# Unsplit 32-bit input projections in a hybrid decoder step, with its parts in another order

## The chip, the cores and the metric

The kernel runs on one core of a Trainium2 chip. The metric is the device time of one execution in microseconds (us); times of a kernel are medians over several runs. The engines of the core are PE (matmul), DVE and POOL (elementwise), ACT (activations) and SP, whose queue issues most of the loads. Each engine takes its instructions strictly in the order in which the program lists them, and waits on semaphores for the others.

## The reference

One inference step of two decoder layers over 256 prompt tokens and 8 single-token samples, width 1024. Cut to what matters here:

```python
def _mixer(h, l, p, st):
    proj = h @ p['w_in'][l]                     # 1024 -> 2968 columns
    z, xbc, dt_raw, rw, gq, gk, gv, glo, gg = _split(proj, IN_SIZES)
    # SSD: causal conv of xbc over 4 tokens, silu, chunked scan, rmsnorm with silu(z)
    # RWKV-7: token shift of rw, decay, delta-rule recurrence, group norm, bonus, gate
    # GLA: log_sigmoid gate from glo, chunked scan, rmsnorm with silu(gg)
    y = jnp.concatenate([y_ssd, y_rwkv, y_gla], axis=-1) @ p['w_out'][l]
...
def _layer(x, c, l, p, st):
    mod = jax.nn.silu(c) @ p['w_ada'][l] + p['b_ada'][l]
    sh1, sc1, gt1, sh2, sc2, gt2 = [m[:, None, :] for m in jnp.split(mod, 6, axis=-1)]
    h = x * (1.0 + sc1) + sh1
    m, new_st = _mixer(h, l, p, st)
    x = _layernorm(ALPHA * x + (1.0 + gt1) * m, p['ln_mix_g'][l], p['ln_mix_b'][l])
    h = x * (1.0 + sc2) + sh2
    f = _swiglu(...) if l % 2 == 0 else _moe(...)
    x = _layernorm(ALPHA * x + (1.0 + gt2) * f, p['ln_ffn_g'][l], p['ln_ffn_b'][l])
    return x, new_st
```

## The kernel before

Activations lie feature by feature: a tile has 128 features in partitions and TT = 264 tokens (256 prompt, 8 samples) in columns, and `h` is four tiles of two such blocks. The stages follow one another: setup and the first `ada` blocks (to about 23 us), mixer of layer 0 (23 to 255), output projection (to about 292), dense FFN (299 to 502), mixer of layer 1 (502 to 697), output projection (to 735), router and experts (741 to 1110), final norm and output.

The large products are made of three fp32r matmuls. `block` (L380) loads a weight tile of 128 x 1024 as `w` through SP's queue (L384), copies it to fp32r on ACT (`wh`, L296) and subtracts that from it on DVE (`wl`, L317). `split` does the same for an activation (`hh`, `hl`). `mm3` (L392) then multiplies wh by hh, wh by hl and wl by hh into one PSUM bank. `tile_mm` (L626) does it for eight k-steps of 128.

In a mixer, `proj` (L680) makes 24 input projections per layer this way (PSUM tile `pj`, two banks): the tiles 0 to 7 are for RWKV, 8 to 13 for the conv of SSD, 14 to 17 for GLA, 18 to 23 for the gates z. Between them run the parts of the mixer: the RWKV chunk chain (`gr`, `pb`, `p`, ...), its single-token step (`rstep`, tiles `sr`, `srw`), its output (`rout`, L1037: `gm`, `gv`, `gn`, `gb`), SSD's preparation (`ssd_prep`, L1231: `ta`, `stk`, `tt`, and a trip through DRAM that comes back as `cu`, from which ACT makes `sd`), its step (`sstep`, L1382: `bx`, `sst`, `sss`), GLA. Interleaved with them, `ada` (L446) makes one block of the adaLN modulation: sixteen matmuls with `wa` tiles, an ACT copy `adae`, four transposes `adat`, and on DVE a reduction, an addition of the bias and sometimes a scaling.

What stands next to what is decided when the program is built. `ORDER` is the order in which a layer's parts are emitted; `LOW` shifts the priority of a named part, projection (`p3.1` is tile 3 of layer 1) or weight split; `FILL` says after which part or projection how many `ada` blocks are emitted. A scheduler turns this into one fixed list of instructions for each engine, so that matmuls of projections fall between the steps of the chains. Buffers are few: three for `w`, three each for `wh` and `wl`, two for `wa`, two PSUM banks for `pj`.

Of the kernel before, what the change touches and what calls it, by code (L numbers as in the profile page):

```python
# [166 lines left out]
def _unpack(r):  # L167
# [20 lines left out]
 'd': 'hh hl cv qk gv zs xo bl xg al',  # L188
# [4 lines left out]
T1 = {'u': 'gt xt x akt rt ee fs raw', 'r': 'vt st vb q1 ab', 'd': 'xb', 't': 'w ends ed sm da dx rs8 mx cslot'}  # L193
# [5 lines left out]
ORDER = [['rwkv', 'conv', 'rstep', 'qkv', 'aff', 'sstep', 'rout', 'gstep', 'gla', 'ssd', 'z2', 'gread', 'z1', 'z0'],  # L199
 ['rstep', 'rwkv', 'conv', 'sstep', 'qkv', 'rout', 'gstep', 'aff', 'gla', 'ssd', 'z0', 'z1', 'z2', 'gread']]  # L200
X = {'FR': 1, 'AHEAD': 1, 'SA': 4}
MOE = {'s0': 28, 'ss': 6, 'g0': 31, 'gs': 5, 'wa': 2, 'e0': 11, 'es': 5}
LOW = {'rout.0': -9440,
 'win.1': -20,
 'sstep.0': -1560,
 'z2.0': -640,
 'rwkv.0': 200,
 'ssd.0': -780,
 'rout.1': -1500,
 'p10.1': 1020,  # L210
 'p4.1': -20,
 'p17.1': -120,
 'sp.1': -20,
 'p0.1': -20,
 'conv.1': -200,
 'win.0': -20,
 'p0.0': -1560,
 'p6.1': -20,
 'gread.1': 100,
 'p16.0': 380,  # L220
 'p14.0': -60,
 'p8.1': -60,
 'fin.1': -60,
 'p19.1': -200,
 'p9.1': 1560,
 'p16.1': 20,
 'p6.0': -20,
 'p9.0': -20,
 'rstep.0': -140,
 'p8.0': -20,  # L230
 'p11.1': -20,
 'p22.0': 200,
 'gp.1': 20}
FILL = {'1.12': 1,
 '1.11': 1,
 '0.13': 1,
 '0.10': 1,
 '1.3': 1,
 '0.qkv': 2,
 '0.o5': 1,  # L240
 '1.z2': 1,
 '0.5': 1,
 '0.15': 1,
 '1.qkv': 1,
 '0.sstep': 1,
 '1.9': 1,
 '1.10': 1,
 '0.conv': 1,
 '0.gla': 1,
 '1.o5': 1,  # L250
 '0.ssd': 1,
 '1.o6': 1}
# [4 lines left out]
ROW = 0  # L257

# [8 lines left out]
class Net:  # L267
    def __init__(self, nc, tc, I, O, stack):
        self.nc, self.tc, self.I, self.O = nc, tc, I, O
        p = lambda name, bufs, **k: stack.enter_context(tc.tile_pool(name=name, bufs=bufs, **k))  # L270
        self.cp = p("const", 1)
        self.wp = p("wts", NW["w"])
        self.ap = p("wada", NW["a"])
        self.hp = p("whi", NW["h"])
        self.lp = p("wlo", NW["l"])
        self.bp = p("big", 1)
        self.p2 = {t: p("f2" + t, n) for t, n in N2.items()}
        self.p1 = {t: p("f1" + t, n) for t, n in N1.items()}
# [123 lines left out]
    def setup(self):  # L402
# [14 lines left out]
        for j in (1, 2, 4, 5):  # L417
            b = self.bada[:, :, j * 8:j * 8 + 8]
            self.ts(b, b, 1.0, OP.add)
# [26 lines left out]
    def ada(self, l, j, n, first=False):  # L446


        if True:
            ps = self.ps("ada")  # L450
            before = None
            for c in range(2):
                cs = slice(c * 256, c * 256 + 256)
                for kq in range(2):
# [6 lines left out]
                    else:  # L461
                        w = self.ap.tile([128, 4, 256], F32, tag="wa", name=f"wa_{self.n}")
                        self.nc.sync.dma_start(w, src)
# [11 lines left out]
            pt = self.ps("adat", [128, 4, 4, 32])  # L475
            for c in range(4):
                self.tr(pt[:, c].rearrange("p a b -> p (a b)"), ev[:, c * 128:c * 128 + 128])
            m = self.mod[:, l, j, n * 4:n * 4 + 4, :]
            self.nc.vector.tensor_reduce(m, pt[:, :, :, :9].rearrange("p c h b -> p c b h"), axis=AX.X, op=OP.add)
            b = self.bada[:, l, j * 8 + n * 4:j * 8 + n * 4 + 4]  # L480
            self.add(m, m, b[:, :, None].to_broadcast([128, 4, 9]))
            if j % 3 == 2:
                self.ts(m, m, 1.0 / ALPHA, OP.mult)
# [26 lines left out]
    def modulate(self, k, gb):  # L510

        gm, bm = gb
        h = self.f2("h")
# [48 lines left out]
    def norm(self, st, g, b, gb=None, keep=False, out=None):  # L562
# [28 lines left out]
        for k, x in zip(range(0, 8, 2), xs):  # L591
            h = self.f2("hk" if keep else "h")
# [40 lines left out]
    def out_proj(self, l, y):  # L633
# [10 lines left out]
        return self.norm(st, g, b, self.scales(l, 3, g, b), l == 1)  # L644

    def ffn(self, l, h):
# [30 lines left out]
        return self.norm(st, g, b, self.scales(l + 1, 0, g, b))  # L677
# [616 lines left out]
    def conv(self, l, h):  # L1294
# [128 lines left out]
    def run(self):  # L1423
        self.setup()
        h, gb = [], self.scales(0, 0)
        for n in range(2):
# [4 lines left out]
            if n == 0:  # L1431
                self.ahead = [self.block(self.I["win"][0, i]) for i in range(X["AHEAD"])]
# [282 lines left out]
```

## Time and profile before

| | us |
|---|---|
| median of 3 runs | 1121.98 |
| runs | 1121.74, 1128.61, 1121.98 |
| profiled execution | 1125.45 |
| its span | 1123.7 |
| PE busy (92%) | 1031.0 |
| DVE busy (66%) | 744.7 |
| ACT busy (54%) | 607.6 |

The mean granted clock of PE in the profiled execution was 0.961 of full speed. Engine time is the time in which the engine had an instruction in work. "Idle before" is the time for which an engine stood still before an instruction; the name after the arrow is the instruction or transfer that released it.

### The profile page before, as it was taken

To read this page: it belongs to the slowest core of one execution; us is meant where nothing else is said; L and a number is where in the kernel's file an instruction comes from. 1 tells how busy PE (TensorE), PEld (TensorE's weight loads), DVE (VectorE), ACT (ScalarE), POOL (GpSimd) and SP (SyncE) were. 2 spreads that over 40 slices of the span, in tenths; PEclk is the share of its full clock that TensorE was granted. 3 is DMA by queue.
4 is the path that set the end of the run, shared out by engine and by line. 5 is a ranking of instruction groups with operands and counts; after the bars stand their busy time and mean duration, and the time that the engine had idled before them with its cause. 6 is when DMAs were issued, how large, how long until landed. Compare 5 with 4: busy or idle time off the path is not lost. (4 is left out here: it accounts for less than half of the span.)

```text
span 1123.7 us, 22379 instructions
## 1 busy us (share of the span) xinstructions
PE 1031.0 (92%) x8912; PEld 833.5 (74%) x8912; DVE 744.7 (66%) x1406; ACT 607.6 (54%) x1037; POOL 87.1 (8%) x191
## 2 busy tenths in 40 slices
PE   6879997889899999999899998979999999999995
PEld 2668765557699999987677875858777777778663
DVE  1577646655665545457876876476788888878775
ACT  2656323254554444338653265357767766776663
POOL 1131112100100000001412210010000000000000
PEclk9999988699899999998999999989999999999998
DMA  9774468773465655555674454416889888988881
GB/s 354 266 220 147 132 205 242 264 232 118 151 194 181 186 176 178 150 169 175 217 226 156 145 170 149 158 43 208 300 296 304 299 286 300 306 291 288 287 280 42
DMA packets 71184, 238.55 MB, mean 212 GB/s; under 512 B 9280, under 2 KB 10016, under 8 KB 71072
## 3 DMA queue, kind: packets, MB, share of 16 engines
q1 hardware_dynamic: 66512, 226.18, 61.4%
q0 software_dynamic: 4000, 10.71, 3.5%
q8 instruction: 72, 1.18, 0.4%
q14 instruction: 40, 0.33, 0.1%
q10 hardware_dynamic: 560, 0.15, 0.1%
HBM read 231.50 MB, written 5.51 MB: 211 GB/s over the span
## 5 line engine op out<-in xcount | busy, mean ns | idle before, releaser
L317 DVE TENSOR_TENSOR wl<-w,wh 128x1024 fp32r<-128x1024 f32 (+1 forms) x324 | 388.7, 1215 | 157.6 <-ACT wh L296 155.5
L296 ACT ACTIVATE wh<-w 128x1024 fp32r<-128x1024 f32 (+1 forms) x324 | 334.2, 1051 | 272.4 <-issue 74.1
L336 PE MATMUL pj<-hh,wh 128*128 128x264 f32 x384 | 119.4, 313 | 7.6 <-ACT cv L296 3.3
L336 PE MATMUL pj<-hl,wh 128*128 128x264 f32 x384 | 120.4, 315 | 0.2 <-DVE hl L317 0.2
L336 PE MATMUL pj<-hh,wl 128*128 128x264 f32 x384 | 118.5, 310 | 1.4 <-DVE wl L317 1.3
L336 PEld LDWEIGHTS pj<-hh,wh 128*128 128x128 f32 x384 | 76.7, 201 | 22.0 <-issue 8.5
L336 PEld LDWEIGHTS pj<-hh,wl 128*128 128x128 f32 x384 | 77.0, 201 | 7.6 <-DVE wl L317 2.7
L336 PE MATMUL eg<-wh,xo 128*128 128x512 f32 x256 | 81.6, 395 | 0.2 <-ACT wh L296 0.2
L336 PEld LDWEIGHTS pj<-hl,wh 128*128 128x128 f32 x384 | 76.7, 200 | 6.7 <-issue 4.0
L336 PE MATMUL eg<-wh,xg 128*128 128x512 f32 x256 | 81.2, 395 | 0.4 <-ACT wh L296 0.4
L336 PE MATMUL ada<-wa,sc 128*32 128x256 f32 x640 | 55.0, 430 | 17.7 <-DMA wa<-in_wada 17.0
L336 PE MATMUL eg<-wl,xg 128*128 128x512 f32 x128 | 53.1, 415 | 5.3 <-DVE wl L317 5.1
L336 PE MATMUL ed<-wl,ath 128*128 128x512 f32 x128 | 52.6, 411 | 4.4 <-DVE wl L317 4.1
L336 PEld LDWEIGHTS eg<-wh,xg 128*128 128x128 f32 x256 | 48.1, 188 | 10.8 <-ACT wh L296 1.4
L336 PEld LDWEIGHTS eg<-wh,xo 128*128 128x128 f32 x256 | 48.1, 188 | 10.3 <-ACT wh L296 0.6
L336 PE MATMUL eg<-wl,xo 128*128 128x512 f32 x128 | 52.5, 410 | 1.5 <-DVE wl L317 1.4
L336 PE MATMUL ed<-wh,ath 128*128 128x512 f32 x128 | 50.9, 398 | 0.0
L336 PE MATMUL ed<-wh,atl 128*128 128x512 f32 x128 | 50.6, 395 | 0.0
L336 PE MATMUL fg<-hh,wh 128*128 128x264 f32 x176 | 50.4, 286 | 0.0
L336 PE MATMUL fu<-hl,wh 128*128 128x264 f32 x176 | 50.4, 286 | 0.0
L336 PE MATMUL fg<-hh,wl 128*128 128x264 f32 x176 | 50.2, 286 | 0.0
L336 PE MATMUL fg<-hl,wh 128*128 128x264 f32 x176 | 50.2, 286 | 0.0
(477 smaller groups left out, 2296.2 us busy)
## 6 DMA issues: line engine op xcount, KB each, us to landing
w<-in_moe SPq DMA_DIRECT2D x192, 512.0 KB, 4.6
wa<-in_wada SPq DMA_DIRECT2D x80, 512.0 KB, 4.5
w<-in_win SPq DMA_DIRECT2D x48, 512.0 KB, 4.6
w<-in_ffgu SPq DMA_DIRECT2D x44, 512.0 KB, 3.6
k<-in_wada SPq DMA_DIRECT2D x32, 256.0 KB, 5.8
w<-in_wout SPq DMA_DIRECT2D x16, 512.0 KB, 4.4
w<-in_ffd SPq DMA_DIRECT2D x16, 512.0 KB, 3.6
w<-in_ffd SPq DMA_DIRECT2D x8, 384.0 KB, 3.9
```

What stands on the lines that cost most here:

```text
L296: r = self.nc.scalar.activation(out, in_, func, bias=bias, scale=scale)
L317: return (e or self.nc.vector).tensor_tensor(out, a, b, op=op)
L336: return self.nc.tensor.matmul(out, lhsT, rhs, start=start, stop=stop)
```

## The change

The projections no longer split weights and input. `raw` loads a weight tile as it is, from the pool of `w`, and `proj` makes eight plain f32 matmuls of the f32 weights and the f32 `h`; `modulate` and the norm after the FFN return `h` unsplit. The other large products (output projection, FFN, experts) stay as they were. The four transposes of `ada` become four f32 matmuls with a 128 x 9 matrix `pick`, which do the sum that the DVE reduction did, and bias and scale are one DVE operation. In the conv, the products for the sample tokens (18 small DVE operations a layer) become one product, one reduction and three additions. In `affine` and the final norm, the product per feature block becomes one per pair, and the gain moves into ACT's scale. The tables ORDER, LOW and FILL have new values; the number of `ada` blocks is the same.

```diff
-ORDER = [['rwkv', 'conv', 'rstep', 'qkv', 'aff', 'sstep', 'rout', 'gstep', 'gla', 'ssd', 'z2', 'gread', 'z1', 'z0'],
- ['rstep', 'rwkv', 'conv', 'sstep', 'qkv', 'rout', 'gstep', 'aff', 'gla', 'ssd', 'z0', 'z1', 'z2', 'gread']]
+ORDER = [['rwkv', 'conv', 'rstep', 'qkv', 'aff', 'sstep', 'rout', 'gstep', 'gla', 'gread', 'ssd', 'z2', 'z1', 'z0'],
+ ['rstep', 'rwkv', 'conv', 'sstep', 'qkv', 'gstep', 'rout', 'aff', 'gla', 'ssd', 'z0', 'z1', 'gread', 'z2']]
...
-LOW = {'rout.0': -9440,
+LOW = {'conv.1': -200,
...
-FILL = {'1.12': 1,
+FILL = {'0.10': 1,
...
+RAW = {'a': 'a', 'p': 'w'}
...
+    def raw(self, src, ada=False):
+
+        self.n += 1
+        c = "a" if ada else "p"
+        kinds = RAW[c]
+        at = self.turn.get(c, 0)
+        self.turn[c] = at + 1
+        k = kinds[at % len(kinds)]
+        pool, tg = {"w": (self.wp, "w"), "a": (self.ap, "wa"), "h": (self.hp, "h"), "l": (self.lp, "l")}[k]
+        w = pool.tile([128, 1024], F32, tag=tg, name=f"w_{self.n}")
+        self.nc.sync.dma_start(w, src)
+        return w
...
-            self.ts(b, b, 1.0, OP.add)
+            self.ts(b, b, 1.0, OP.add, *((1.0 / ALPHA, OP.mult) if j % 3 == 2 else ()))
+        self.pick = cp.tile([128, 9], F32, name="pick")
+        nc.vector.tensor_reduce(self.pick, self.ident.rearrange("p (q b) -> p b q", q=4)[:, :9], axis=AX.X, op=OP.add)
         self.mod = cp.tile([128, L, 6, 8, 9], F32, name="mod")
...
-                        w = self.ap.tile([128, 4, 256], F32, tag="wa", name=f"wa_{self.n}")
-                        self.nc.sync.dma_start(w, src)
+                        w = self.raw(src, True).rearrange("p (a b) -> p a b", a=4)
                         ws = [w[:, :2], w[:, 2:]]
...
-            pt = self.ps("adat", [128, 4, 4, 32])
+            pt = self.ps("adat", [128, 4, 9])
             for c in range(4):
-                self.tr(pt[:, c].rearrange("p a b -> p (a b)"), ev[:, c * 128:c * 128 + 128])
+                self.mm(pt[:, c], ev[:, c * 128:c * 128 + 128], self.pick)
             m = self.mod[:, l, j, n * 4:n * 4 + 4, :]
-            self.nc.vector.tensor_reduce(m, pt[:, :, :, :9].rearrange("p c h b -> p c b h"), axis=AX.X, op=OP.add)
-            b = self.bada[:, l, j * 8 + n * 4:j * 8 + n * 4 + 4]
-            self.add(m, m, b[:, :, None].to_broadcast([128, 4, 9]))
+            b = self.bada[:, l, j * 8 + n * 4:j * 8 + n * 4 + 4, None].to_broadcast([128, 4, 9])
             if j % 3 == 2:
-                self.ts(m, m, 1.0 / ALPHA, OP.mult)
+                self.stt(m, pt, 1.0 / ALPHA, OP.mult, b, OP.add)
+            else:
+                self.add(m, pt, b)
...
-        h = self.f2("h")
+        h = self.f2("hw")
         self.act(h[:, 0, :T], self.x[:, k, :T], AF.Identity, scale=gm[:, k, 0:1], bias=bm[:, k, 0:1])
         self.ts(h[:, 1, :T], self.x[:, k + 1, :T], gm[:, k + 1, 0:1], OP.mult, bm[:, k + 1, 0:1], OP.add)
         self.mul(h[:, :, T:], self.x[:, k:k + 2, T:], gm[:, k:k + 2, 1:], self.nc.gpsimd)
         self.add(h[:, :, T:], h[:, :, T:], bm[:, k:k + 2, 1:], self.nc.gpsimd)
-        r = self.f2("hh", dt=F32R), self.f2("hl", dt=F32R)
-        self.split(r[0], r[1], h)
-        return r
+        return h
...
+                self.mul(y, y, r[:, None, :].to_broadcast([128, 2, TT]))
                 for i in range(2):
-                    self.stt(y[:, i], y[:, i], g[:, k + i:k + i + 1], OP.mult, r, OP.mult)
-                    self.act(y[:, i], y[:, i], AF.Identity, bias=b[:, k + i:k + i + 1])
+                    self.act(y[:, i], y[:, i], AF.Identity, scale=g[:, k + i:k + i + 1], bias=b[:, k + i:k + i + 1])
...
-            h = self.f2("hk" if keep else "h")
+            h = self.f2(keep or "h")
...
-            for k in range(8):
-                x = self.x[:, k]
-                both = self.stt(x, x, g[:, k:k + 1], OP.mult, r, OP.mult), self.act(x, x, AF.Identity, bias=b[:, k:k + 1])
+            for k in range(0, 8, 2):
+                x = self.x[:, k:k + 2]
+                both = [self.mul(x, x, r[:, None, :].to_broadcast([128, 2, TT]))]
+                for i in range(2):
+                    both.append(self.act(x[:, i], x[:, i], AF.Identity, scale=g[:, k + i:k + i + 1], bias=b[:, k + i:k + i + 1]))
...
     def proj(self, l, i, h):
         with self.low(f"p{i}.{l}"):
-            hi, lo = self.ahead.pop(0) if self.ahead else self.block(self.I["win"][l, i], by=f"win.{l}")
+            w = self.ahead.pop(0) if self.ahead else self.raw(self.I["win"][l, i])
             ps = self.ps("pj")[:, :TT]
-            self.tile_mm(ps, hi, lo, h)
+            for k in range(8):
+                self.mm(ps, w[:, k * 128:k * 128 + 128], h[k // 2][:, k % 2], k == 0, k == 7)
...
+        old, S3 = self.f1("cvt", [128, 6, NB]), [128, 6, 3, NB]
+        each = self.f1("cve", S3)
+        self.mul(each, scv, cw[:, :, :3, None].to_broadcast(S3))
+        nc.vector.tensor_reduce(old, each.rearrange("p t k b -> p t b k"), axis=AX.X, op=OP.add)
...
-                self.stt(yq[:, T:], scv[:, t, k], w(k), OP.mult, yq[:, T:], OP.add)
...
+                self.add(y[:, :, T:], y[:, :, T:], old[:, t - 1:t + 1])
...
-                self.ahead = [self.block(self.I["win"][0, i]) for i in range(X["AHEAD"])]
+                self.ahead = [self.raw(self.I["win"][0, i]) for i in range(X["AHEAD"])]
```

The new order shows on three engines. First ACT in mixer 0, at the r and v projections of RWKV; `tt` belongs to the preparation of SSD, `sd` needs the transfer `cu`, and `ab` goes to the RWKV chain. Before:

```order
L296 ACTIVATE v_468<-pj_705,omu 128x264
L296 ACTIVATE adae_683<-ada_658 128x512
L296 ACTIVATE raw_767<-pj_742 128x264
L296 ACTIVATE v_468<-pj_742,omu 128x264
L296 ACTIVATE ta_777<-ta_777 8x256
L296 ACTIVATE wh_1580<-w_1578 128x1024
L296 ACTIVATE tt_799<-stk_798 128x144
L296 ACTIVATE sd_806<-cu_805,tt_799 128x128 x4
L296 ACTIVATE lt_849<-lg_848 128x264
L296 ACTIVATE sd_806<-sd_806 128x512
L296 ACTIVATE lt_849<-lt_849 128x264
L296 ACTIVATE ab_869<-gr_894 128x128
```

After:

```order
L308 ACTIVATE b_465<-b_465 128x264 x2
L308 ACTIVATE tt_619<-stk_618 128x144
L308 ACTIVATE r_409<-pj_494,omu 128x264
L308 ACTIVATE r_409<-pj_511,omu 128x264
...
L308 ACTIVATE v_410<-pj_561,omu 128x264
L308 ACTIVATE raw_587<-pj_578 128x264
L308 ACTIVATE v_410<-pj_578,omu 128x264
L308 ACTIVATE sd_626<-cu_625,tt_619 128x128 x4
L308 ACTIVATE ab_689<-gr_714 128x128
```

`tt` stood behind the v projections, directly ahead of `sd`, and now stands ahead of both r and v; `sd` is still ahead of `ab`, by one place. Then DVE in mixer 0, where the step of SSD meets the output of RWKV; `sst` needs the transfer `bx`, and `gn` goes to PE for `gv` and `gb`. Before:

```order
L333 SCALAR_TENSOR_TENSOR o_589<-gm_2263,o_589 128x264
L317 TENSOR_TENSOR sss_2200<-sss_2200,da_844 128x512
L317 TENSOR_TENSOR sst_2175<-bx_2170,dx_2159 128x2x128 x2
L333 SCALAR_TENSOR_TENSOR gn_2261<-r_467,par,k_109_564 128x264
L317 TENSOR_TENSOR sss_2174<-sss_2174,sst_2175 128x512
L317 TENSOR_TENSOR wl_2962<-w_2959,wh_2961 128x1024
```

After:

```order
L345 SCALAR_TENSOR_TENSOR o_491<-gm_1862,o_491 128x264
L329 TENSOR_TENSOR sss_1801<-sss_1801,da_664 128x512
L345 SCALAR_TENSOR_TENSOR gn_1860<-r_409,par,k_101_466 128x264
L329 TENSOR_TENSOR sst_1776<-bx_1771,dx_1760 128x2x128 x2
L329 TENSOR_TENSOR sss_1775<-sss_1775,sst_1776 128x512
L329 TENSOR_TENSOR gn_1860<-gb_1872,v_410 128x264
```

`gn` stood behind `sst` and now stands ahead of it. Last SP's queue of loads in mixer 0, with what each load waits for (`w` are projection weights when they come from in_win, `wada` the weights of `ada`). Before:

```order
L384 DMA w_1491<-in_win 128x1024 [waits DMAHW5_49,DVE_49]
L384 DMA w_1533<-in_win 128x1024 [waits DMAHW7_49,DMAHW6_49,DVE_49]
L463 DMA wa_671<-in_wada 128x1024 [waits PE_49]
L463 DMA wa_677<-in_wada 128x1024 [waits DMAHW0_49,PE_49]
L463 DMA wa_1610<-in_wada 128x1024 [waits DMAHW7_49,DMAHW1_49,PE_49]
L384 DMA w_1578<-in_win 128x1024 [waits DMAHW2_49,DVE_49,Activation_49]
L463 DMA wa_1616<-in_wada 128x1024 [waits DMAHW3_49,DMAHW0_49,PE_49]
L384 DMA w_1655<-in_win 128x1024 [waits DMAHW4_49,DMAHW5_49,DVE_49,Activation_49]
L384 DMA w_1699<-in_win 128x1024 [waits DMAHW6_49,DVE_49,Activation_49]
```

After:

```order
L414 DMA w_1357<-in_win 128x1024 [waits DMAHW5_49,PE_49]
L414 DMA w_1409<-in_win 128x1024 [waits PE_49]
L414 DMA w_1431<-in_win 128x1024 [waits DMAHW7_49,DMAHW2_49,PE_49]
L414 DMA w_1450<-in_win 128x1024 [waits DMAHW5_49,PE_49]
L414 DMA w_1381<-in_wada 128x1024 [waits DMAHW1_49,PE_49]
L414 DMA w_1387<-in_wada 128x1024 [waits DMAHW3_49,PE_49]
L414 DMA w_1473<-in_wada 128x1024 [waits DMAHW1_49,PE_49]
L414 DMA w_1479<-in_wada 128x1024 [waits DMAHW4_49,DMAHW2_49,PE_49]
L414 DMA w_1613<-in_win 128x1024 [waits DMAHW6_49,PE_49]
```

A load of projection weights waited for DVE (and ACT), which had split the tile in its buffer, and now waits for PE, which has multiplied with it; the loads of `ada` are in the same queue, in groups, as before.

## Rows read from the trace of the kernel before

**Rows 1.** The page's first part: busy us, share of the span, instructions of an engine.

```profile
PE 1031.0 (92%) x8912; PEld 833.5 (74%) x8912; DVE 744.7 (66%) x1406; ACT 607.6 (54%) x1037; POOL 87.1 (8%) x191
```

**Rows 2.** Windows: width, busy us of PE, PEld, DVE, ACT, POOL, clock, DMA share, GB/s.

```profile
23.00:255.00 232.00, 204.32 (x2581) 152.66 (x2582) 140.76 (x344) 103.44 (x229) 35.41 (x69) 0.90 0.67 218
...
299.00:502.00 203.00, 203.00 (x1623) 196.99 (x1625) 109.24 (x160) 93.21 (x139) 0.00 (x0) 0.99 0.56 170
502.00:697.00 195.00, 178.58 (x2399) 142.26 (x2392) 147.12 (x364) 106.50 (x241) 40.12 (x76) 0.96 0.57 181
```

**Rows 3.** Waits of PE: its instruction <- releaser, us in total, times, longest.

```profile
PE ada L336 <- DMA wa<-in_wada: 17.0, 13, 3.5
...
PE adat L369 <- ACT adae L296: 5.4, 8, 0.8
...
PE pb L369 <- DVE x L317: 5.0, 1, 5.0
...
PE gb L336 <- DVE gn L333: 4.4, 1, 4.4
...
PE pj L336 <- ACT cv L296: 3.3, 1, 3.3
```

**Rows 4.** Timeline, all engines, at 78 us: start, us, engine, instruction [idle before <- releaser].

```profile
78.56 1.28 ACT L296 ACTIVATE sd<-cu,tt 128x128 f32<-128x128 f32 x4 [5.73 <-DMA cu<-ssdd]
...
80.89 0.25 ACT L296 ACTIVATE ab<-gr 128x128 f32<-128x128 f32 x1
...
81.25 0.29 DVE L317 TENSOR_TENSOR x<-gr,cst 128x128 f32<-128x128 f32 x1 [6.11 <-ACT ab L296]
...
81.59 0.48 PE L369 MATMUL pb<-ident,b 128*128 128x128 f32 x1 [5.01 <-DVE x L317]
```

**Rows 5.** Timeline, all engines, at 177 us.

```profile
176.92 0.76 DVE L317 TENSOR_TENSOR sst<-bx,dx 128x256 f32<-128x256 f32 x2 [4.69 <-DMA bx<-bcr_d]
...
178.14 0.81 PE L336 MATMUL gb<-gn,cst 128*128 128x264 f32 x1 [4.44 <-DVE gn L333]
```

**Rows 6.** Timeline of PE, at 50 and at 254 us.

```profile
49.75 0.28 PE L336 MATMUL pj<-hh,wl 128*128 128x264 f32 x1
...
53.90 0.28 PE L336 MATMUL pj<-hh,wh 128*128 128x264 f32 x1
...
254.05 1.05 PE L336 MATMUL ssq<-zs,onem 128*128 128x264 f32 x4
254.94 0.61 PE L336 MATMUL gn<-gsq,cst 128*128 128x264 f32 x2
```

**Rows 7.** The page's groups: busy us, mean ns of one | idle before.

```profile
L317 DVE TENSOR_TENSOR wl<-w,wh 128x1024 fp32r<-128x1024 f32 (+1 forms) x324 | 388.7, 1215 | 157.6 <-ACT wh L296 155.5
L296 ACT ACTIVATE wh<-w 128x1024 fp32r<-128x1024 f32 (+1 forms) x324 | 334.2, 1051 | 272.4 <-issue 74.1
```

**Rows 8.** Timeline, at 33 and (PE) at 760 us.

```profile
32.95 0.66 PE L369 MATMUL adat<-ident,adae 128*128 128x128 f32 x4 [0.76 <-ACT adae L296]
...
759.73 1.66 PE L336 MATMUL cs<-comb,sel 128*128 128x1 f32 x12
```

**Rows 9.** Timeline, all engines, at the start of mixer 0.

```profile
34.22 1.09 ACT L296 ACTIVATE h<-x,mod 128x256 f32<-128x256 f32 x2 [1.32 <-DVE mod L317]
...
35.22 1.16 ACT L296 ACTIVATE hh<-h 128x528 fp32r<-128x528 f32 x2
...
35.89 0.59 PE L336 MATMUL pj<-hh,wh 128*128 128x264 f32 x1 [2.29 <-ACT hh L296]
```

**Rows 10.** Loads: the page's DMA issues, the issuing line (ns, landing us), SP's waits.

```profile
w<-in_win SPq DMA_DIRECT2D x48, 512.0 KB, 4.6
...
L384 SPq DMA_DIRECT2D w<-in_win x48: 327/328/1538, 14.3 to 644.7; - x48
...
DMA to landing us min/median/max: 3.1/4.5/8.2
...
SPq L463 <- PE ada L336: 127.9, 57, 11.7
```

More of the change, by code (lines that the diff above doesn't have):

```diff
@@ L187 @@
 T2 = {'r': 'ai k r cs kk k2 ka rkt bk gn gr ah htl az',
- 'd': 'hh hl cv qk gv zs xo bl xg al',
+ 'd': 'hh hl hw cv qk gv zs xo bl xg al',
  'g': 'gqk gsc o hk sq rbt',
@@ L192 @@
  'm': 'srm srv bx sst sgu sgl gsq'}
-T1 = {'u': 'gt xt x akt rt ee fs raw', 'r': 'vt st vb q1 ab', 'd': 'xb', 't': 'w ends ed sm da dx rs8 mx cslot'}
+T1 = {'u': 'gt xt x akt rt ee fs raw', 'r': 'vt st vb q1 ab', 'd': 'xb', 't': 'w ends ed sm da dx rs8 mx cslot cvt'}
 TP = {'a': 'ada adat st',
@@ L198 @@
 N1 = {'r': 10, 'd': 2, 's': 8, 't': 13, 'u': 6}
-ORDER = [['rwkv', 'conv', 'rstep', 'qkv', 'aff', 'sstep', 'rout', 'gstep', 'gla', 'ssd', 'z2', 'gread', 'z1', 'z0'],
- ['rstep', 'rwkv', 'conv', 'sstep', 'qkv', 'rout', 'gstep', 'aff', 'gla', 'ssd', 'z0', 'z1', 'z2', 'gread']]
+ORDER = [['rwkv', 'conv', 'rstep', 'qkv', 'aff', 'sstep', 'rout', 'gstep', 'gla', 'gread', 'ssd', 'z2', 'z1', 'z0'],
+ ['rstep', 'rwkv', 'conv', 'sstep', 'qkv', 'gstep', 'rout', 'aff', 'gla', 'ssd', 'z0', 'z1', 'gread', 'z2']]
 X = {'FR': 1, 'AHEAD': 1, 'SA': 4}
-MOE = {'s0': 28, 'ss': 6, 'g0': 31, 'gs': 5, 'wa': 2, 'e0': 11, 'es': 5}
-LOW = {'rout.0': -9440,
- 'win.1': -20,
[L205 to L233, printed above, removed]
-FILL = {'1.12': 1,
[L235 to L241, printed above, removed]
- '0.5': 1,
[L243 to L247, printed above, removed]
+MOE = {'e0': 11, 'es': 5, 'g0': 31, 'gs': 5, 's0': 28, 'ss': 6, 'wa': 2}
+LOW = {'conv.1': -200,
+ 'fin.1': -80,
+ 'gp.1': 40,
+ 'gread.0': -600,
+ 'gread.1': 100,
+ 'p0.0': -1560,
+ 'p0.1': -20,
+ 'p10.1': 1020,
+ 'p11.1': -20,
+ 'p13.1': -1520,
+ 'p14.0': -60,
+ 'p14.1': 200,
+ 'p16.1': 20,
+ 'p17.1': -120,
+ 'p19.1': -200,
+ 'p21.0': 60,
+ 'p22.0': 200,
+ 'p4.1': -20,
+ 'p6.0': -20,
+ 'p6.1': -20,
+ 'p7.0': -600,
+ 'p8.0': -20,
+ 'p8.1': -60,
+ 'p9.0': -20,
+ 'p9.1': 1560,
+ 'rout.0': -9440,
+ 'rout.1': -1500,
+ 'rp.0': 60,
+ 'rp.1': 20,
+ 'rstep.0': -140,
+ 'rstep.1': 20,
+ 'rwkv.0': 200,
+ 'sp.1': -20,
+ 'ssd.0': -780,
+ 'sstep.0': -1560,
+ 'win.1': -20,
+ 'wout.1': -60,
+ 'z0.1': -20,
+ 'z1.1': -1500,
+ 'z2.0': -640}
+FILL = {'0.10': 1,
+ '0.15': 1,
+ '0.5': 1,
  '0.conv': 1,
  '0.gla': 1,
- '1.o5': 1,
+ '0.o5': 1,
+ '0.qkv': 2,
+ '0.rstep': 1,
  '0.ssd': 1,
- '1.o6': 1}
+ '0.sstep': 1,
+ '1.12': 1,
+ '1.18': 1,
+ '1.3': 1,
+ '1.9': 1,
+ '1.o4': 1,
+ '1.o6': 1,
+ '1.qkv': 1,
+ '1.ssd': 1,
+ '1.z1': 1,
+ '1.z2': 1}
 NW = {'w': 3, 'a': 2, 'h': 3, 'l': 3}
@@ L283, in __init__ @@
         self.setname = None
+        self.turn = {}
         self.pre = None
@@ L643, in out_proj @@
         g, b = self.P(l, "lnm_g"), self.P(l, "lnm_b")
-        return self.norm(st, g, b, self.scales(l, 3, g, b), l == 1)
+        return self.norm(st, g, b, self.scales(l, 3, g, b), "hk" if l == 1 else None)
     def ffn(self, l, h):
@@ L676, in ffn @@
         g, b = self.P(l, "lnf_g"), self.P(l, "lnf_b")
-        return self.norm(st, g, b, self.scales(l + 1, 0, g, b))
+        return self.norm(st, g, b, self.scales(l + 1, 0, g, b), "hw")
     def proj(self, l, i, h):
         with self.low(f"p{i}.{l}"):
-            hi, lo = self.ahead.pop(0) if self.ahead else self.block(self.I["win"][l, i], by=f"win.{l}")
+            w = self.ahead.pop(0) if self.ahead else self.raw(self.I["win"][l, i])
             ps = self.ps("pj")[:, :TT]
-            self.tile_mm(ps, hi, lo, h)
+            for k in range(8):
+                self.mm(ps, w[:, k * 128:k * 128 + 128], h[k // 2][:, k % 2], k == 0, k == 7)
         self.hook(l, i)
```

## The prediction

> **What bounds the kernel now.** I read the engine table first: TensorE (PE) is busy 92% of the span, and its weight loads 74% [rows 1]. Then the table by stage [rows 2]. In the dense FFN between the two mixers PE has no idle time at all (203.00 of 203.00 us), so nothing that the change does there could show, and it does almost nothing there. The two mixers are the only stages where PE both works hard and waits: in the first it is busy 204.3 of 232 us, in the second 178.6 of 195, which leaves 27.7 + 16.4 = 44.1 us idle, and the granted clock is 0.90 and 0.96 where the FFN has 0.99. All the projections lie in these stages. So the change is a trade on one engine: more matmul time in the mixers, against whatever part of the 44.1 us (and of the low clock) is caused by the work that it removes.
>
> Third, the list of PE's waits, to see what those 44.1 us are [rows 3]. The largest is not the projections at all but `ada` waiting for its own weights (17.0 us in 13 waits). Then come two single long stalls of 5.0 and 4.4 us, and small waits for ScalarE (ACT) and VectorE (DVE). The two long ones are worth following in the timeline. At 81.59 PE's transpose `pb` begins after 5.01 us idle; it waits for a DVE product that waits for `ab` on ACT; and ACT stood 5.73 us before `sd`, which needs `cu`, a DMA through DRAM of the SSD part [rows 4]. `ab` was ready to go and stood behind `sd`. The second is the same on DVE: `sst` waited 4.69 us for the DMA `bx`, and the product `gn`, which PE's `gb` needs, stood behind it [rows 5]. Both are head-of-line stalls of an in-order engine, not lack of throughput.
>
> **The change, part by part.** *Projections.* A product of three fp32r matmuls has its starts 122 ns apart (49.75 to 53.90 in 34 steps [rows 6]), so a k-step costs 366 ns and a tile of eight 2.93 us. The new product is one f32 matmul, which PE runs as two passes. The nearest row is `ssq`, f32 with the same 264 columns: four passes from 254.05 to the next operation at 254.94, 222 ns each [rows 6]. Two passes are 445 ns, a tile 3.56 us. 48 tiles of eight products: 384 x 0.079 = **+30 us**. The far ends would be a pass as cheap as an fp32r one (0.122, -47 us) and one of twice that (0.244, +47); the first is excluded by the `ssq` row, which has the same type, shape and accumulation and which I take, and +47 stays as a bound. [...]
>
> *What no longer runs.* 48 ACT copies of 1.05 us and 48 DVE subtractions of 1.22 us [rows 7]: 50 us of ACT and 59 us of DVE, in stages where each was busy about half the time or somewhat more [rows 2]. With the split of `h` and the small conv operations, DVE and ACT get lighter by a quarter or so. None of this is on the path by itself; it counts only through PE's waits below.
>
> *`ada`.* Four transposes and a DVE reduction become four f32 matmuls with nine columns, eight passes. Four transposes took 0.66 us; twelve f32 passes of one column took 1.66 us, at most 0.14 each [rows 8]. Eight passes are up to 1.1 us, so +0.45 a block, and some 20 blocks (of 24; the first four stand before mixer 0) lie beside PE work: **+9 us**, which is the upper bound; the lower is 0, where such a block fills a wait. DVE saves a reduction per block, which nothing on the path waits for once the next block's fill comes in between.
>
> *Conv, affine, final norm.* Fewer, wider DVE operations with the same bytes. They are hidden behind PE work; in the final norm, where nothing hides them, four multiplications replace eight products and ACT's eight operations stay. I cost them at nothing, half a microsecond either way.
>
> *The two stalls.* In the new ACT order the SSD preparation (`tt`) stands ahead of the r and v projections, so `cu` should have landed long before `sd` reaches the head. In the new DVE order `gn` stands ahead of `sst`. I take both whole, -5.0 and -4.4: **-9.4 us**; late next there are the projections, on PE itself. If either DMA is still late elsewhere, half comes back.
>
> *Starts.* Mixer 0's first product waited 2.29 us for the `hh` copy that begins at 35.22 [rows 9]; without it the products can begin with `h`, and the following tiles are not paced by `hl`: **-2.5 us**. In mixer 1 the same pacing is worth about **-1.5**.
>
> *The other waits.* `ada` on its DMA 17.0, and about 15 us of the rest of the 44.1 (`adat`, `cv`, and many under 1 us) [rows 3]. The two engines named are the ones that lose work, and a longer projection tile gives each load more time. I take 70% of 32: **-22 us**; bounds 0 and 32.
>
> *Clock.* 10% of 232 us and 4% of 195 is 31 us of lost clock [rows 2], an upper bound, since PE was waiting in part of it; I take 13 as really lost, and 70% of it back with the stalls that precede slow stretches: **-9 us**, bounds 0 and 31.
>
> *Switches.* The projections come in a few less pieces between waits: -1.
>
> *Loads.* A weight buffer used to be free when the DVE subtraction was done, three split tiles ahead of PE; now only after PE's last product on it. With three buffers a load goes out when two tiles are left, 2 x 3.56 = 7.1 us of work; issue and landing take 0.33 + 4.6 us [rows 10]. That leaves 2.2 us, and I cost it at nothing; the rival below is what happens without that cover.
>
> The sum: +30 + 9 - 9.4 - 2.5 - 1.5 - 22 - 9 - 1 = -6.4 us. The profiled execution took 1125.45 us (span 1123.7 and 1.75 around it), 3.5 above the median of 1121.98; from it the sum gives 1119, from the median 1115.6. The time asked for is one like the median: **1115**.
>
> **Rivals.** *Nearly all of the idle time goes.* With ACT and DVE this much lighter and a fresh order, PE could run the mixers as densely as the FFN. Then all 44 us of idle and the 13 of clock go: 1122 + 38 - 57 = **1103**. For it: the FFN row shows that PE can be kept full by the same loads. Against: `ada` waits on a DMA, which neither engine feeds.
>
> *The projection weights run dry (slower).* SP issues `w` and `wa` loads in one in-order queue, and a `wa` row waits until PE has used an older one: 127.9 us in 57 waits, 2.2 us each and up to 11.7 [rows 10]. That is just the slack worked out above. It decides where a tile follows tile without other PE work: eight at the start of mixer 0, eleven and a half at the start of mixer 1 in the new order. If the loads there land as late as the longest seen, 8.2 + 0.33 us against 7.1, each tile waits 1.4 us: 19.5 x 1.4 = +27, and the whole is **1142**. From a landing of about 6.8 us on, the queue decides. For it: the buffers are freed later than before. Against: the median load lands in 4.5 us, and the mixers' DMA share is 0.57 to 0.67, not full.
>
> [...]
>
> **How the numbers follow.** A measurement of this kernel can tell about 1% (11 us) from no change. Chances: my sum (1104 to 1127) 0.42, of which 0.06 lies below 1110.8; nearly all idle gone 0.34; weights run dry 0.18; four intervals 0.06. Faster by over 1%: 0.34 + 0.06 = 0.40. Slower: 0.18. The same: 0.36 + 0.06 = 0.42. The range that leaves out about 0.1 at each end runs from 1096, below the second case (the whole clock bound could go too), to 1137, inside the third.
>
> **What would show it.** In the profile of the changed kernel: `pj` with 768 records, starts about 222 ns apart in a dense stretch, and 3.56 us from tile to tile; the idle time before `pb` and `gb` under 1 us each; first `pj` at about 33.5 to 34.5 us; PE's waits for wa under 10 us in total; mixer windows with PE idle near 18 us together instead of 44, and a clock of 0.95 or more in both. I would be wrong if `pj` shows waits for a DMA of `w` of more than a few us (third case), if passes are 244 ns apart, or if PE's idle time stays near 44 us because other waits take the place of those removed.

## The result, and the profile after

The changed kernel is slower: 1161.77 us (median of 4) against 1123.79 in the same comparison, a ratio of 1.032 with a 95% interval of 1.024 to 1.040. The profiled execution took 1158.62 us, with a span of 1156.8, which is 33.1 more than before. The prediction said 1115, a little faster, with a range up to 1137: the change went the other way, and beyond the range. Times of kernels are medians; a ratio is an estimate over the runs of a comparison and can differ from the quotient of two medians by some tenths of a percent.

First the engine totals of the changed kernel, from the first part of its page (busy us, share of the span, instructions):

```profile
PE 1079.3 (93%) x8624; PEld 838.5 (72%) x8624; DVE 675.0 (58%) x1269; ACT 566.2 (49%) x981; POOL 80.8 (7%) x191
```

DVE and ACT lost 70 and 41 us of work, as foreseen; PE gained 48 [rows 1], and only 15 of these came out of its idle time. The windows of its two mixers and the FFN between them (width, busy us of PE, PEld, DVE, ACT, POOL, then clock, DMA share, GB/s):

```profile
21.90:264.80 242.90, 226.02 (x2422) 151.87 (x2422) 107.51 (x286) 79.26 (x198) 31.35 (x69) 0.93 0.61 198
314.40:518.10 203.70, 203.70 (x1621) 197.61 (x1625) 104.82 (x148) 91.02 (x132) 0.00 (x0) 0.99 0.55 165
518.10:727.40 209.30, 198.29 (x2247) 142.55 (x2246) 116.22 (x304) 89.00 (x220) 38.16 (x76) 0.95 0.54 169
```

Against [rows 2] the mixers are 10.9 and 14.3 us wider, with 24% and 19% less DVE and ACT work in them. PE's idle time there fell from 44.1 to 16.9 + 11.0 = 27.9 us. That is a gain of 16 where the prediction had counted on some 35 (stalls 9.4, starts 4, other waits 22), before a single microsecond for the clock. The FFN is unchanged. I also cut the two executions at the first `pj`, the first `op` and the first `fg` or the last `fd`, and added PE's time from each start to the next:

| | before | after |
|---|---|---|
| mixer 0, first `pj` to first `op` | 231.9 | 242.9 |
| output projection 0, to the first `fg` | 43.9 | 49.5 |
| mixer 1, last `fd` to the second `op` | 195.7 | 209.3 |
| the rest, with the FFN and the experts | 652.2 | 655.1 |
| `pj` on PE, both mixers | 182.0 | 212.1 |
| `adat` on PE, mixers and output projections | 12.2 | 21.3 |

The two terms of PE work came out: `pj` +30.1 us where 30 was predicted, `adat` +9.1 where 9 was (10.0 with the blocks ahead of mixer 0 and behind the second output projection). The other 8 us of added PE time are spread over many operations. The projection group of the page:

```profile
L348 PE MATMUL pj<-hw,w 128*128 128x264 f32 x768 | 224.1, 429 | 2.4 <-POOL hw L329 2.3
```

And a dense run of eight passes in the timeline (start, us):

```profile
262.41 1.94 PE L348 MATMUL pj<-hw,w 128*128 128x264 f32 x8
```

The last of the eight passes takes 0.386 us of the 1.94, so starts lie (1.94 - 0.386) / 7 = 0.222 us apart, the number taken from `ssq` [rows 6]. The projections never wait for a weight load: 2.3 of their 2.4 us are POOL's part of `h`. So what failed is nearly everything with a minus sign. PE's waits, and SP's, answering to [rows 3] and [rows 10]:

```profile
PE ada L348 <- DMA w<-in_wada: 14.2, 9, 3.2
...
PE gv L348 <- ACT gn L308: 4.5, 1, 4.5
...
PE adat L348 <- ACT adae L308: 4.1, 6, 0.8
...
SPq L414 <- PE pj L348: 183.5, 34, 10.4
SPq L414 <- PE ada L348: 104.2, 50, 9.0
```

`ada`'s wait for its weights is still there (14.2 instead of 17.0), and SP now stands 183.5 us before loads that wait for PE's projections. The stall of 5.0 us before `pb` is gone: ACT is still busy with the v projections when `cu` lands, and `sd` has nothing to wait for. The one of 4.4 before `gb` has moved by one product, to `gv`:

```profile
81.31 0.49 ACT L308 ACTIVATE v<-pj,omu 128x264 f32<-128x264 f32 x1
81.67 1.28 ACT L308 ACTIVATE sd<-cu,tt 128x128 f32<-128x128 f32 x4
...
180.91 0.76 DVE L329 TENSOR_TENSOR sst<-bx,dx 128x256 f32<-128x256 f32 x2 [5.07 <-DMA bx<-bcr_d]
...
182.66 0.42 DVE L345 SCALAR_TENSOR_TENSOR o<-gm,o 128x264 f32<-128x264 f32 x1
...
183.11 0.42 ACT L308 ACTIVATE gn<-o 128x264 f32<-128x264 f32 x1 [6.62 <-DVE o L345]
...
183.59 1.25 PE L348 MATMUL gv<-gn,cst 128*128 128x264 f32 x2 [4.52 <-ACT gn L308]
```

`gn` for the first half now runs ahead of `sst`, and the `o` from which ACT makes the next `gn` stands behind it, waiting for the same transfer. That transfer went out later, too: POOL issued `bx` at 170.54 us before and at 175.17 now.

### The profile page after: what moved, and what is told of

It is laid out like the page before. It is cut to its first block, busy times and chain, and to the rows that moved or that the text cites. A ratio compares the mean times of both kernels' runs of the same rounds, so it can differ in the third digit from the quotient of the medians.

```text
span 1156.8 us, 21591 instructions
## 1 busy us (share of the span) xinstructions
PE 1079.3 (93%) x8624; PEld 838.5 (72%) x8624; DVE 675.0 (58%) x1269; ACT 566.2 (49%) x981; POOL 80.8 (7%) x191
## 4 chain that ended last, share of the span: by engine, by line
PE 60%; DMA 22%; DVE 8%; ACT 6%; issue 3%; POOL 0%; SPq 0%; ACTq 0%; DVEq 0%; POOLq 0%
PE pj L348 15%; DMA w<-in_moe 14%; PE fd L348 6%; PE fg L348 6%; DVE wl L329 6%; PE fu L348 6%; ACT wh L308 4%; PE op L348 4%; PE ada L348 4%; DMA w<-in_wada 3%; PE p L348 3%; PE ed L348 2%; DMA bx<-bcr_d 2%; PE adat L348 2%; PE eg L348 2%
## 5 line engine op out<-in xcount | busy, mean ns | idle before, releaser
L329 DVE TENSOR_TENSOR wl<-w,wh 128x1024 fp32r<-128x1024 f32 (+1 forms) x276 | 330.2, 1215 | 152.9 <-ACT wh L308 151.3
L308 ACT ACTIVATE wh<-w 128x1024 fp32r<-128x1024 f32 (+1 forms) x276 | 283.6, 1050 | 217.9 <-issue 72.5
L348 PE MATMUL pj<-hw,w 128*128 128x264 f32 x768 | 224.1, 429 | 2.4 <-POOL hw L329 2.3
L348 PEld LDWEIGHTS pj<-hw,w 128*128 128x128 f32 x768 | 145.6, 204 | 44.7 <-issue 13.7
L348 PE MATMUL ada<-w,sc 128*32 128x256 f32 x640 | 52.7, 415 | 14.5 <-DMA w<-in_wada 14.2
L348 PE MATMUL fu<-hh,wh 128*128 128x264 f32 x176 | 50.4, 286 | 0.0
L348 PE MATMUL fu<-hh,wl 128*128 128x264 f32 x176 | 50.3, 286 | 0.0
L348 PE MATMUL fd<-bh,wl 128*128 128x264 f32 x160 | 45.7, 286 | 0.0
L348 PE MATMUL fd<-bl,wh 128*128 128x264 f32 x160 | 45.7, 286 | 0.0
```

Of the source, the lines that this page charges most:

```text
L308: r = self.nc.scalar.activation(out, in_, func, bias=bias, scale=scale)
L329: return (e or self.nc.vector).tensor_tensor(out, a, b, op=op)
L348: return self.nc.tensor.matmul(out, lhsT, rhs, start=start, stop=stop)
```

## Experiments: the parts, each in the order that the scheduler then makes

My theory after the result was that PE's added passes are paid in full. The rivals were that the new tables cost the time, and that the small parts (pick, conv, affine) do. `raw_only` puts `raw`, the eight f32 products and the unsplit `h` into the kernel before; `small_only` puts in everything else except the tables; `old_tables` and `split_again` undo one thing in the changed kernel:

```diff
 (old_tables)
-ORDER, LOW, FILL of the changed kernel
+ORDER, LOW, FILL of the kernel before
 (split_again)
-            w = self.ahead.pop(0) if self.ahead else self.raw(self.I["win"][l, i])
+            hi, lo = self.ahead.pop(0) if self.ahead else self.block(self.I["win"][l, i], by=f"win.{l}")
...
+            self.tile_mm(ps, hi, lo, h)
```

> The kernel before with one part of the change: unsplit weights and input and f32 projections; tables, ada, conv and affine as before. If the loss is PE time in the projections (30 us of passes in the trace of the changed kernel, little of it given back), about 1140 to 1150 against 1124 before. If the new tables cost it, about 1115 to 1125, since the old tables then suit the lighter DVE and ACT. PE's pj time up by 30 us in either case.

> The kernel before with the other part alone: the four f32 matmuls with pick in ada, the wider conv, affine and final norm; projections split and tables as before. If passes on PE are what counts, adat adds about 9 us and the saved DVE operations give back a few: 1124 to 1133. If DVE work in the mixers holds PE up, faster than before: 1112 to 1120.

> The changed kernel with ORDER, LOW and FILL of the kernel before. If PE time is the loss, as slow as the changed kernel: 1150 to 1165, or slower, since the new tables were to fit it. If the new tables are the loss (projections of z last, the tail before the output projection), 1125 to 1135.

> The changed kernel, new tables and all, with split weights and three fp32r products per step in the projections again. If PE time of the f32 passes is the loss, about 30 us under the changed kernel: 1125 to 1135. If the tables are the loss, 1145 to 1160.

Measured, each against the kernel before on the same chip (1125.5 us): raw_only 1141.7, ratio 1.015 (1.008 to 1.022); small_only 1156.3, 1.023 (1.013 to 1.033); old_tables 1161.1, 1.033 (1.026 to 1.040); split_again 1162.3, 1.031 (1.024 to 1.039). The tables are worth nothing measurable either way: the theory of the tables falls. But the theory of the f32 passes alone falls too, since taking them out of the changed kernel gains nothing. In split_again's profile `pj` is 24.5 us shorter than in the changed kernel (187.7 for 212.2), but PE's idle time in the mixers is 45.7 us instead of 27.9, and its mean clock over the runs 0.939 instead of 0.962: there, the relief of DVE and ACT and the clock do pay for the passes. And raw_only's `pj` grew by 19 us, not by the 30 that I expected. My theory had not held the small parts for expensive. The next four take those apart. `pick_only` changes only the second half of `ada` in the kernel before, `conv_only` the conv, affine and final norm, `twice_tr` adds as many passes as pick does, and `no_pick` undoes pick in the changed kernel:

```diff
 (pick_only)
-                self.tr(pt[:, c].rearrange("p a b -> p (a b)"), ev[:, c * 128:c * 128 + 128])
+                self.mm(pt[:, c], ev[:, c * 128:c * 128 + 128], self.pick)
 (twice_tr)
-            for c in range(4):
+            for c in (0, 1, 2, 3, 0, 1, 2, 3):
```

> The kernel before with only the four f32 matmuls with pick in ada in place of four transposes and the DVE reduction. If they cost their own passes alone, adat's PE time rises by about 9 us and the time to 1130 to 1134 against 1124; if they also pull PE's granted clock down (0.94 instead of 0.96, as with all the small parts together), 1140 to 1155; if it was the conv and affine parts, no change.

> The kernel before with only the wider conv, affine and final norm operations; ada with its transposes, projections split, tables as before. If pick is the cost of the small parts, 1118 to 1126. If the new conv and affine order is what delays the mixers, 1135 to 1150.

> The kernel before with each of ada's transposes made twice: the same added PE time as pick (eight passes a block instead of four, about 9 us in all), but of transposes and without another change on DVE. If PE time is what counts, about 1130 to 1134; if pick's own kind of matmul lowers the clock, this keeps 0.96 and pick_only does not; if the added passes lower the clock whatever they are, both do.

> The changed kernel with only ada's transposes, reduction and scaling put back. If pick costs what the small parts cost together, 1130 to 1140 against 1162 of the changed kernel; if only its passes, about 1152; if it costs nothing, 1160.

Measured against 1126.9: pick_only 1153.8, ratio 1.026 (1.021 to 1.030); conv_only 1133.7, 1.005 (1.002 to 1.009); twice_tr 1142.5, 1.016 (1.012 to 1.021); no_pick 1145.6, 1.017 (1.012 to 1.021). Pick costs 27 to 29 us alone and 16 to 17 in the changed kernel (by medians and by ratios), for 9 us of passes. The same number of passes as transposes costs 16 to 18, more than the 1130 to 1134 that I expected, at an unchanged clock; in its profile PE's idle time in the mixers is 51.3 us instead of 43.8. The granted clock (mean over the runs of each kernel) says where some of it went: 0.946 with pick alone, 0.94 with all small parts, 0.961 with double transposes, 0.968 with the f32 projections alone, 0.969 without pick in the changed kernel, 0.939 without the f32 projections in it, 0.962 in the changed kernel, 0.96 before. So the two parts go with opposite shifts of the clock, and their costs don't add: 17 + 29 + 6 would be 52, the change is 36 to 38.

These runs share a weakness. conv_only takes work off DVE, adds none on PE and is 6 us slower. Any edit lets the scheduler move other instructions: in the traces of the five edits of the kernel before, some 120 to 215 of PE's 3917 stretches of like matmuls no longer stand in its sequence. A cost of 6 us may be no more than such a shift; conv was not run with the order held.

## Experiments: one edit, with the order held

So I held the order. Up to the router, each engine's instructions are chained by order-only edges into the sequence of the kernel before, read from its built program (PLACES); an edited step stands where the step that it replaces stood. One engine is left out in held_raw, held_raw_split and held_raw_buffers: there SP's loads keep the order that the scheduler makes. Of 176 loads of projection and `ada` weights, some 30 stand elsewhere in held_raw than before, and some 20 elsewhere again in held_raw_buffers. PE's sequence in the traces is that of before in all of them, but for the products that were replaced.

```diff
+    def pin(self):
...
+        t = json.loads(zlib.decompress(base64.b85decode(PLACES)))
+        got = self.places()
...
+                for i in q[at]:
+                    if last is not None:
+                        self.tc.add_manual_dep(i, last.name, mybir.DependencyInfo(
+                            mybir.DependencyClass.NoSync, mybir.DependencyReason.DATA), reason="place")
+                    last = i
...
 (held_pick_wide, and held_after_wide)
+            self.pick = cp.tile([128, 128], F32, name="pick")
...
+            nc.gpsimd.memset(self.pick[:, 9:], 0.0)
 (held_raw_buffers, raw_buffers, after_buffers)
-RAW = {'a': 'a', 'p': 'w'}
+RAW = {'a': 'a', 'p': 'whl'}
```

> The kernel before, with its own order of instructions held by explicit order-only edges on every engine up to the router, so that an edit can no longer move other instructions. A control: as the kernel before, 1120 to 1130.

> The same held order, with ada's four f32 matmuls with pick in the place of the four transposes. If pick costs only its passes, +9 us: 1130 to 1136 against 1125. If what cost the other 15 to 20 us in pick_only was pick itself (a lower clock), 1145 to 1155; if it was the shifted order, this run is near 1133.

> As held_pick, with pick padded by zeros to 128 columns: the same eight passes a block, whose cost is the weight load, but as many columns as the transposes had. If thin matmuls pull the granted clock down, the clock returns to 0.96 and the time falls from 1145 to about 1135. If it is the number of passes or another thing, it stays at 1140 to 1150.

> The same held order (loads left free), with each three fp32r products replaced by one f32 product at the place of the first, and no splits. If PE's added passes are paid in full less the idle time that the lighter DVE and ACT give back by themselves, 1135 to 1150; if my sum was right and only the new order spoiled it, 1100 to 1120.

> As held_raw, but the 48 ACT copies and 48 DVE subtractions of the weights are still made, with nobody reading them: the relief of DVE and ACT taken away again. If that relief is worth what my sum says (22 us of waits, 9 of clock), 20 to 30 us slower than held_raw. If PE's idle time in the mixers has other causes, within 5 us of it.

> As held_raw, but the projection weights take turns in three pools (w, and those of wh and wl), nine buffers instead of three. If SP's in-order queue of loads holds ada's loads back behind projection loads that wait for PE, ada's waits fall from 27 us to 15 or less and the time from 1155 to 1140 to 1147. If the queue is not the cause, no change.

| kernel | us | ratio to before | 95% interval |
|---|---|---|---|
| held_before | 1126.95 | 1.000 | 0.997 to 1.004 |
| held_pick | 1144.69 | 1.018 | 1.011 to 1.024 |
| held_pick_wide | 1133.86 | 1.006 | 1.002 to 1.009 |
| held_raw | 1155.29 | 1.026 | 1.020 to 1.031 |
| held_raw_split | 1164.92 | 1.036 | 1.031 to 1.040 |
| held_raw_buffers | 1142.39 | 1.011 | 1.008 to 1.015 |

The control holds: the edges themselves cost nothing that could be measured. Then three readings.

**Pick is thin.** Padded with zeros it does the same eight passes a block and costs 6 us instead of 19. (The doubled transposes, as many passes in an order left free, cost 16 to 18.) A block of eight passes in the timeline of held_pick, then of held_pick_wide:

```profile
72.90 0.95 PE L339 MATMUL adat<-pick,adae 128*128 128x9 f32 x8
```

```profile
68.15 1.05 PE L339 MATMUL adat<-pick,adae 128*128 128x128 f32 x8
```

Their two mixers in the windows (columns as above), in the same order:

```profile
23.30:261.50 238.20, 217.27 (x2629) 164.92 (x2630) 137.42 (x328) 103.60 (x229) 36.20 (x69) 0.87 0.64 212
510.40:713.90 203.50, 184.78 (x2432) 148.45 (x2431) 145.71 (x355) 107.30 (x243) 39.30 (x76) 0.95 0.55 174
```

```profile
23.30:250.90 227.60, 205.22 (x2631) 157.68 (x2631) 137.69 (x328) 103.38 (x229) 34.50 (x69) 0.93 0.66 222
498.30:704.80 206.50, 188.08 (x2431) 151.00 (x2431) 145.99 (x355) 107.41 (x243) 38.97 (x76) 0.93 0.54 171
```

A block of 9 columns is even 0.1 us shorter (in the trace of the changed kernel the eight weight loads of such a block take 1.07 us from 260.86 on, its passes 0.96 from 261.07), and the kernel 11 us longer by the medians (13 by the ratios). What differs is the clock. In mixer 0 of these two executions it was 0.87 of full speed with thin passes and 0.93 with wide ones. PE's busy time there is 12 us longer with the thin passes, its idle time 1.5 us shorter. Mixer 1 goes the other way, by less (0.95 with thin passes and 0.93 with wide ones, 3 us shorter), so one stage of one execution proves nothing; the evidence is the mean clock of all runs, 0.947 for the four of held_pick (0.943 to 0.954) and 0.964 for the ten of held_pick_wide (0.961 to 0.969). The free orders agree: pick_only and twice_tr, with eight passes a block of 9 and of 128 columns, are 11 us and 0.015 of clock apart. Over all 24 blocks the passes keep PE about as long in both kernels (25.4 and 25.9 us), so their time does not tell them apart; the measured clocks do. Why the clock differs is not shown.

**The f32 passes.** held_raw is 1.0256 x 1126 - 1126 = 29 us slower. That this is close to the 30 of the prediction is in part chance. Its mixers, after those of held_before:

```profile
23.30:251.80 228.50, 204.98 (x2582) 153.54 (x2583) 141.44 (x344) 103.39 (x229) 35.92 (x69) 0.91 0.66 221
498.80:694.30 195.50, 180.20 (x2403) 142.82 (x2402) 148.30 (x365) 107.23 (x242) 39.64 (x76) 0.96 0.57 181
```

```profile
22.30:268.40 246.10, 221.10 (x2393) 146.81 (x2391) 113.30 (x316) 80.17 (x203) 30.40 (x68) 0.90 0.63 207
517.00:725.40 208.40, 191.53 (x2210) 136.09 (x2209) 120.73 (x330) 86.09 (x217) 35.02 (x76) 0.97 0.55 172
```

PE's busy time there grew by 27 us, 22 of them `pj` (181.3 to 203.4), and its idle time did not shrink (38.8 to 41.9 us): nothing of the passes was covered. The relief of DVE and ACT does count: making the 48 copies and subtractions again, unread, costs another 10 us (held_raw_split; 1.0356 against 1.0256). The prediction had 31 for it (22 of waits, 9 of clock). Longer waits of `ada`, next, took part of it back.

**The loads.** With PE's order held, its wait of `ada` for its weights grew, though of `ada` only the places of its loads in SP's queue had changed. First PE's wait in held_before, then PE's and SP's waits of held_raw, then of held_raw_buffers:

```profile
PE ada L338 <- DMA wa<-in_wada: 19.6, 15, 3.5
```

```profile
PE ada L341 <- DMA wa<-in_wada: 27.1, 19, 3.5
...
SPq L407 <- PE pj L341: 178.9, 37, 14.1
```

```profile
PE ada L341 <- DMA wa<-in_wada: 20.8, 11, 4.8
...
SPq L407 <- PE pj L341: 136.2, 25, 14.1
```

With nine buffers for the projection weights SP waits less for PE, `ada` waits 6 us less, and the kernel gains about half of the 29 (13 us between the medians, 16 between the ratios). So here the queue of loads was a cost, not to the projections, which waited for no load, but to `ada`, whose loads stand behind theirs. How large a cost is not shown: the waits fell to 20.8 us, not to the 15 expected, SP's order changed along with the buffers, and in held_raw_split, with held_raw's loads and three buffers, `ada` waits only 18.3 us. In the orders that the scheduler makes by itself the same buffers gave nothing:

> raw_only (order left to the scheduler) with the same nine buffers. If the queue is the cause, 1142 falls to 1125 to 1135. If not, no change beyond what a shifted order does, about 6 us either way.

> The changed kernel with the same nine buffers and nothing else. If the queue is the cause, ada's 14 us of waits fall below 7 and the time from 1162 to 1145 to 1153; if not, 1155 to 1165.

raw_buffers 1145.65, ratio 1.017 (1.013 to 1.021), against raw_only's 1.015; after_buffers 1166.53, 1.031 (1.026 to 1.037), against 1.032. `ada` waits 18.2 and 20.5 us in them, against 18.9 and 14.2 without the buffers. There the queue was not the cause.

Last, two single terms: pick padded in the changed kernel with its own order held, and the two stalls of [rows 4] and [rows 5] taken out of the order of the kernel before, by moving rows of the held order alone (ACT's `ab` ahead of the four `sd`; DVE's `sst` pair and `sss` behind both `gn` and the second `o`).

> The changed kernel with its own order held on every engine, and only pick padded by zeros from 9 to 128 columns. If thin matmuls lower the clock here as they did in the held order of before, 1162 falls by 8 to 13 us, to 1149 to 1154, at a clock above that of the changed kernel; if not, 1158 to 1165.

> The kernel before in its held order, with only this moved: ACT's ab ahead of the four sd that wait for the transfer cu, and DVE's sst and sss behind the two gn and the o that PE waits for. If the two stalls are worth what my sum took, 9 us faster: 1113 to 1119 against 1126. If another wait takes their place, within 4 us of 1126.

held_after_wide took 1154.12 us, ratio 1.020 (1.014 to 1.027), mean clock 0.970 instead of 0.962. Against 1.032 that is 13 us less by the ratios and 8 by the medians, for columns of zeros; the two intervals overlap, and the changed kernel was not run with its order held and pick thin, so this is less sure than in the held order of before. held_moved took 1129.87, ratio 1.003 (1.000 to 1.006): nothing gained. First the two places in the profile of held_before, which is its control, then in its own:

```profile
83.31 0.33 PE L371 MATMUL pb<-ident,b 128*128 128x128 f32 x1 [3.46 <-DVE x L319]
...
175.38 0.76 DVE L319 TENSOR_TENSOR sst<-bx,dx 128x256 f32<-128x256 f32 x2 [0.18 <-DMA bx<-bcr_d]
```

```profile
78.53 1.28 ACT L299 ACTIVATE sd<-cu,tt 128x128 f32<-128x128 f32 x4 [4.46 <-DMA cu<-ssdd]
...
81.45 0.43 DVE L336 SCALAR_TENSOR_TENSOR lg<-lg,lt 128x264 f32<-128x264 f32 x1 [5.80 <-ACT lt L299]
...
84.63 0.48 PE L339 MATMUL gr<-sg,ka 64*64 64x64 f32 x4 [4.76 <-DVE x L320]
...
190.72 0.76 DVE L320 TENSOR_TENSOR sst<-bx,dx 128x256 f32<-128x256 f32 x2 [4.16 <-DMA bx<-bcr_d]
...
192.94 0.99 PE L339 MATMUL gg<-gqk 32*32 32x32 f32 x64 [3.94 <-DVE gqk L320]
```

`pb` and `gb` no longer wait. But `sd` still waits on ACT, `lt` behind it, DVE's `lg` for `lt`, the next `x` behind `lg`, and PE stops 4.76 us before `gr`. The next `sst` waits on DVE ahead of `gqk`, and PE stops 3.94 us before `gg`. The instruction that was named had changed; the late transfer had not. The control shows one thing more: with the very order of before, `bx` had landed by the time `sst` came (0.18 us, not 4.69), and `gb` waited for nothing. The stall of 4.4 us was not a matter of the order alone.

## Why the prediction was wrong, point by point

- **The sum:** in the two profiled executions PE's busy time grew by 48.3 us (`pj` 30, `adat` 10, the rest in small pieces) and its idle time fell by 15.2. The prediction had 39 of work and 45 to be given back. The step that failed is the giving back.
- **Projections +30, ada's passes +9:** right for the changed kernel, and the 0.222 us between passes was right. That `pj` came out to 0.1 us is luck: at the dense intervals it would be 140.5 us before and 170.9 now, and the 41 us on top of that, at the lower clock (in the trace of before `pj` passes start 0.22 us apart from 82.73 to 85.81 us, at a granted clock of 0.50, and 0.122 in the dense stretch) and at the seams, happen to be the same in both. In raw_only and held_raw the same edit added 19 and 22 us. No run shows the "four intervals" of the chances (0.06): `pj` has 768 records for 384 products, 0.222 us apart.
- **ada, the size of its effect:** the term was mis-sized. It counted passes (9) and not the clock that went with them (0.947 over the runs of held_pick, 0.964 padded): 19 us in the held order, 6 when padded. Nothing in the trace of before showed thin passes in a stretch that mattered, and no end of the range allowed for it.
- **The two stalls -9.4:** the step "I take both whole" failed. One went: the first `cu` landed 2.3 us earlier (at 76.2 us, not 78.5), and `sd` came to the head of ACT's list only at 81.67. The other moved by one product. held_before shows that the 4.4 us are not always there in that order, and held_moved that moving both out of the way is worth nothing while the transfers stay late. The sentence in the prediction that they are "head-of-line stalls, not lack of throughput" was true and no reason to count them as gain.
- **The other waits -22:** the step that failed most. The waits were to shrink because DVE and ACT lose work; most of them were `ada` waiting for a load that neither engine feeds, which the prediction itself says against its fast rival. PE's idle time in the mixers fell by 16 us for stalls, starts and waits together, against 35 counted; without the stalls and the `hh` wait, by 11 against 22. The 17.0 us of `ada` were also not all in the mixers: 14.4 of them were, and 11.4 are left there now.
- **Clock -9:** not seen. A stall ahead of a slow stretch is in the trace of before (PE idle for 5.01 us up to 81.59, a granted clock of 0.50 from 80.3 to 87.1 us, 1.00 from 70 to 80.3 and from 87.1 to 100), but the mean did not rise. The profiled clock is 0.961 before and after; with pick alone it is 0.946, with the f32 products alone 0.968.
- **Starts -4:** one of the 4 was seen. In mixer 0 the wait for `hh` (2.29 us) became one of 1.13 for POOL's part of `h`, and the block ahead of it ended later.
- **Loads at nothing:** the slack of 2.2 us was enough for the projections, as worked out. What the step left out is who stands behind them in SP's queue. In the changed kernel that shows no cost (`ada` waits no longer than before, and nine buffers gave nothing); in held_raw it does. The slower rival named the right queue, but not the operation that waits.
- **The tail of mixer 0** was not in the sum at all. The last projections of z ended at 242 us before and end at 264 now, after the scan's last `py` at 254, so that the norm of the SSD output runs beside the first output projections, and that stage grew by 5.6 us; 24 more of `ada`'s matmuls stand in it, too. By old_tables, which has 45.9 us there and the same total, this order is not what decides.

What stays open: in the free orders I can bound the parts (raw 0 to 17, pick 16 to 29, conv 6, each with an unknown shift of the order in it), but not add them up to the 36 to 38 of the change, and no run with the order held has raw and pick together against the kernel before. Which orders of `ada`'s loads would keep them off PE's path was not tried. No version beat the kernel before.

## What to carry to other kernels

Where one engine is busy nine tenths of the time, work added to it is certain and the idle time that other engines' relief gives back is a hope (here PE was busy 92%, 48.3 us were added and 15.2 of idle time came back): count the first in full, and the second only for waits whose releaser really loses work, followed to the transfer at its head. When instructions move in order past a late transfer, look for the next one that stands behind it; moving the name in the trace is not removing the wait. And to price one edit of a scheduled kernel, hold the order of everything else, or run an edit that should be free beside it.

## What was not expected of the hardware

The matmuls with 9 moving columns cost more than their own time here: eight passes of 9 columns (0.95 us) in place of eight of 128 (1.05 us), in 24 blocks, went with a mean granted clock of 0.947 over the runs instead of 0.964 and made the kernel 11 us longer, with the same order of instructions. In the other direction, replacing three fp32r matmuls of 0.122 us by two f32 passes of 0.222 went with a higher clock in the free order (0.968 against 0.96); whether it is these passes that raised it was not isolated, and in the held order it stayed at 0.962.
